# A macaron attention layer on one core: the differential softmax shared out over three engines, and the output projection as four plain products

## The chip, the core and the metric

The kernel runs on one core of one Trainium2 chip. The metric is the device time of one execution in microseconds (us), the median of a few runs. The core has TensorE (PE, matrix products; PEld is its weight load), VectorE (DVE), ScalarE (ACT), GpSimd (POOL) and SyncE (SP, which issues most DMAs). Each engine takes its instructions in the order in which the program lists them; waits between engines go through semaphores.

## The reference, cut to what matters

One layer on x of 1024 rows by 1024 columns, float32: a half-step SwiGLU block, two attentions side by side whose outputs are gated, summed and projected, and a second half-step SwiGLU block.

```python
# B: differential attention, 4 heads, two score maps per head
p = jax.nn.softmax(sc, axis=-1)
attn = p[:, :, 0] - lam * p[:, :, 1]
return jnp.einsum('bhqk,bkhe->bqhe', attn.astype(v.dtype), v)
...
g_a, g_b = jnp.split(jax.nn.sigmoid(gate_logits + b_gate[li]), 2, axis=-1)
merged = g_a * (y_a @ w_branch_a[li]) + g_b * (y_b @ w_branch_b[li])
x = x + merged @ w_o[li]
x = x + 0.5 * swiglu_ffn(rms_norm(x, ffn2_norm[li]), ffn2_w_in[li], ffn2_w_out[li])
```

Attention A has 8 heads of 64 over a band of 576 keys, attention B sees all chunks up to its own.

## The kernel before

**Products.** A float32 product is made of three reduced-precision ones: each operand is split into a high and a low part, and `mm3` (lines 129 to 133) issues hi*hi, lo*hi and hi*lo into one accumulator. The split (lines 96 to 110) is a cast on ScalarE (L100) and a difference on VectorE (L105). The large projections use the seven-product scheme of Strassen and Winograd: sums of operand blocks (A11, S1, ...; B11, T1, ...) are formed first, then seven products instead of eight.

**Order.** The framework takes the program's operations, simulates them with costs of its own, and from that sets the order on each engine and the buffer of each tile. So a change in one place can move instructions around it. The buffers that matter here are pools of fixed size: 14 `big` tiles, 10 `raw`, 10 `f`, and in PSUM 6 banks `mm` and 2 each of `tr`, `pt`, `pv`; the attention's scores take two `sc` tiles of two banks.

**Attention.** The work is cut into jobs that run as a pipeline of five (function `run`). 32 jobs of attention A (4 head pairs, 4 row blocks, 2 heads) are mixed with 16 jobs of attention B (heads 0 and 1); then come the 16 B jobs of heads 2 and 3, with steps of the branch A projection as filler. A job's first step makes scores on TensorE (L783, L784), subtracts them from the bias and takes the minimum on VectorE (L791), and takes exp and its row sum on ScalarE (L793). Two steps later the probabilities are transposed on TensorE (L799, PSUM tile `pt`), split (L100, L105), and multiplied with v (L870, L958).
- An A job has two row blocks; for each, VectorE takes the reciprocal of the row sum (L853) and GpSimd scales the probabilities (L854).
- A B job has two maps r = 0, 1 of up to 1024 keys (128, 256, ..., 1024 for its row block i = 0 to 7). VectorE takes both reciprocals (L939, L941), forms r2 = -lam * sum0 / sum1 (L942), and adds the second map to the first: pr[0] = pr[1] * r2 + pr[0] (L944). The first reciprocal is applied later, on the small result (L961, L963). GpSimd then adds the two halves (L964) and makes two small operations of the norm (L142, L970).

**Merge and output projection.** For each pair jj of 128-column blocks TensorE projects branch B (tile `pb`), VectorE gates it and adds branch A's part (L1027, L116). The result is kept in the seven operand sums that the scheme needs (A11, A12, A22 and S1 to S4): S1 and S2 are formed on VectorE, S3 and S4 on GpSimd (L1036, L1037). `out_projection` (lines 430 to 520) then does w_o in the order P1, P2, P6, P5, P3, P7, P4, four steps of 48 matmuls each, with the sums of weight blocks (T1, T2, ...) formed on VectorE between them; each product is added to the rows of x by VectorE (L510). The same function does the projections of both SwiGLU blocks, in another order.

**Behind it.** When both halves of the upper 512 rows are complete, `early` normalises them and transposes them (L208) into A11 and A12. When the lower rows are complete, `mid` and `late` do theirs: five `head`s of the next SwiGLU block, which need only A11 and A12, are issued between the normalisation of the lower rows and the sums S1, S2, S4 that the rest needs (`norm1a`).

Of the kernel before, what the change touches and what calls it, by code (L numbers as in the profile page):

```python
# [9 lines left out]
F32 = mybir.dt.float32  # L10
# [47 lines left out]
def hybrid_layer_kernel(ctx, tc, x, ffn1_norm, ffn1_w_in, ffn1_w_out, mix_norm, w_mix_in,  # L58
# [35 lines left out]
    nc.vector.memset(neg_half, -0.5)  # L94

# [257 lines left out]
    def ffn_in(w_in, u, ps, extra=None):  # L353
# [51 lines left out]
        for j, p in enumerate(pairs):  # L405
# [13 lines left out]
           "P7": ("S3", "T3", "q", 1, 1)}  # L419
    FFN_ORDER = ("P1", "P5", "P6", "P3", "P7", "P2", "P4")  # L420
    WO_ORDER = ("P1", "P2", "P6", "P5", "P3", "P7", "P4")
# [6 lines left out]
    WO_LOADS = {(0, 0): (("B11", 0, 4), ("B21", 0, 4), ("B12", 0, 4), ("B22", 0, 4))}  # L428

    def out_projection(w_out, operand, order, loads, scale, x_src, x_dst, ps,  # L430
# [5 lines left out]
        wv = w_out.rearrange("(i two p) d -> two p i d", two=2, p=P)  # L436
# [5 lines left out]
        def load_block(name, i0, i1):  # L442
            n = 2 if name == "B11" else 4
            for j0 in range(i0, i1, n):
                r = min(n, i1 - j0)
                b = raw_tile([P, 2, HALF], name) if n == 2 else big([P, 4, HALF], name, F32)
                nc.sync.dma_start(out=b[:, :r], in_=wv[int(name[1]) - 1][
                    :, j0:j0 + r, (int(name[2]) - 1) * HALF:int(name[2]) * HALF])
                for i in range(r):
                    blocks[name, j0 + i] = b[:, i, :]  # L450

        def weight(name, i):

            b11, b12, b21, b22 = (blocks.get((n, i)) for n in ("B11", "B12", "B21", "B22"))
            if order == WO_ORDER and name == "T2":
                add(b11, b12, b11, ALU.subtract)
                t2 = wtemp([P, HALF], "T2")
                add(t2, b22, b11, ALU.subtract)
                add(b21, b21, t2, ALU.subtract)
                return t2  # L460
            if order == FFN_ORDER and name in ("T1", "T2"):
# [17 lines left out]
        for m, name in enumerate(order):  # L479
# [3 lines left out]
            if first:  # L483
                banks[chain] = [ps.tile([P, HALF], F32, tag=tag, bufs=n, name="po") for tag, n in
                                (("mm", 6), ("mm", 6)) + ((("mm", 6),) * 2 if chain == "q" else (("tr", 2),) * 2)]
            if m == len(order) - 1 and last:
                early()
            for i in range(nk):
# [3 lines left out]
                if order == FFN_ORDER and bn == "B21":  # L492
# [261 lines left out]
    with tc.tile_pool(name="ps2", bufs=1, space=PSUM) as ps:  # L754
# [71 lines left out]
        def jobs_a(pr):  # L826
# [8 lines left out]
            def job(sb_, h):  # L835
# [9 lines left out]
                pms = []  # L845
                for s, i in enumerate((i0, i1)):
# [68 lines left out]
        def jobs_b(hb, filler):  # L915
# [10 lines left out]
            def job(i):  # L926
# [3 lines left out]
                pr, rs = [], []  # L930
                for r in range(2):
                    sc, n = scores(qkv, r, i, 0, w)
                    pm = raw_tile([P, WB], "pm")[:, :w]
                    s_ = small.tile([P, 1], F32, tag="rs", name="rs")
                    softmax(sc, n, nb[:, WB - w:], pm, s_)
                    pr.append(pm)
                    rs.append(s_)
# [74 lines left out]
    with tc.tile_pool(name="ps3", bufs=1, space=PSUM) as ps:  # L1012


        mo = {n: big([P, 4, HALF], f"m{n}", F32) for n in U_OPS}
        for jj in range(KT // 2):
            wr = load(w_cols(w_branch_b[0], jj * 256, 256, 0, 4), raw_tile([P, 4, 256]))
            for odd in range(2):
                j = 2 * jj + odd
                w = split_units(wr[:, :, odd * P:(odd + 1) * P], branch_unit)  # L1020
                for th in range(2):
# [6 lines left out]
                    if (odd, th) == (0, 1):  # L1028
                        a21 = ta
                    else:  # L1030
                        m = mo["A12" if odd and not th else "A22" if odd else "A11"][:, jj, :]
                    add(a21 if (odd, th) == (0, 1) else m, gl, ta)
# [69 lines left out]
```

## Time and profile before

| | us |
|---|---|
| three runs | 2160.55, 2162.82, 2162.94 (median 2162.82) |
| the profiled execution | 2162.35, of which 2160.5 are its span |
| TensorE busy | 2079.4, 96% of the span |
| VectorE, ScalarE, GpSimd busy | 1463.7, 977.7, 189.6 |

The profile is of one execution. Busy time of TensorE counts a matmul to its modelled end, so matmuls that follow each other overlap; what one costs in a row of them is the distance between two starts. A row's "idle before" names what ended the wait. Line numbers are those of the kernel before.

### The profile page before, as it was taken

How to read it: one execution, taken by the hardware profiler on the slowest of the kernel's cores; microseconds unless marked ns; L12 is line 12 of the kernel's file. 1: busy time of each engine (PE TensorE's matmuls, PEld its weight loads, DVE VectorE, ACT ScalarE, POOL GpSimd, SP SyncE). 2: the span in 40 equal slices, each digit the busy share in tenths (PEclk: the TensorE clock that was granted, in tenths of full speed). 3: DMA queues.
4: the chain of work that ended last, by engine and by line, in shares of the span. 5: the costliest groups of instructions: out<-in, count | busy, mean ns of one | idle time of the engine just before them, and what ended most of it. 6: DMA issues, size and time to landing. Idle time of an engine off the chain costs nothing.

```text
span 2160.5 us, 29119 instructions
## 1 busy us (share of the span) xinstructions
PE 2079.4 (96%) x10025; PEld 1733.3 (80%) x10025; DVE 1463.7 (68%) x2678; ACT 977.7 (45%) x1911; POOL 189.6 (9%) x290
## 2 busy tenths in 40 slices
PE   6999999999999999999988999998999999999997
PEld 5788888888888788899777787776788888888886
DVE  7666566577577756566588986777765665658566
ACT  5433333334446444444487864135433333334444
POOL 2120000000001000000065432101000000000001
PEclk9999999999999999999999999999999999999999
DMA  6653333294344645553785567614643333366334
GB/s 193 175 170 108 98 98 112 93 348 125 117 139 149 178 134 169 191 186 137 244 296 202 189 226 238 237 59 156 180 144 96 111 98 98 117 237 226 98 114 160
DMA packets 285157, 348.24 MB, mean 161 GB/s; under 512 B 16221, under 2 KB 171885, under 8 KB 284113
## 3 DMA queue, kind: packets, MB, share of 16 engines
q1 hardware_dynamic: 283680, 342.62, 48.4%
q0 software_dynamic: 1184, 3.24, 0.6%
q8 instruction: 79, 1.29, 0.3%
q14 instruction: 70, 0.57, 0.1%
q10 hardware_dynamic: 144, 0.52, 0.1%
HBM read 233.79 MB, written 112.53 MB: 160 GB/s over the span
## 4 chain that ended last, share of the span: by engine, by line
PE 81%; DVE 9%; DMA 3%; issue 3%; ACT 2%; SPq 0%; POOL 0%; ACTq 0%; DVEq 0%; POOLq 0%
PE prod L131 19%; PE prod L132 19%; PE prod L133 18%; PE po L132 6%; PE po L133 6%; PE po L131 6%; DVE wlo L105 3%; DVE pm L791 2%; PE pb L131 1%; PE pb L133 1%; PE pb L132 1%; PE tr L208 1%; DVE B L116 1%; PE pt L799 1%; ACT whi L100 1%
## 5 line engine op out<-in xcount | busy, mean ns | idle before, releaser
L132 PE MATMUL po<-wlo,whi 128*128 128x512 f32 x728 | 284.8, 391 | 5.7 <-DVE wlo L105 5.4
L133 PE MATMUL po<-whi,wlo 128*128 128x512 f32 x728 | 283.5, 389 | 0.0
L100 ACT CAST whi<-raw 128x512 fp32r<-128x512 f32 x200 | 124.4, 622 | 312.6 <-PE prod L132 245.5
L100 ACT CAST whi<-T 128x512 fp32r<-128x512 f32 x196 | 121.8, 622 | 249.8 <-PE prod L132 227.4
L100 ACT CAST whi<-B 128x512 fp32r<-128x512 f32 x178 | 110.8, 623 | 266.0 <-PE po L132 258.0
L116 DVE TENSOR_TENSOR c<-prod,c 128x512 f32<-128x512 f32 x190 | 131.1, 690 | 134.9 <-PE prod L133 122.3
L105 DVE TENSOR_TENSOR wlo<-raw,whi 128x512 fp32r<-128x512 f32 x200 | 138.6, 693 | 106.0 <-ACT whi L100 65.0
L105 DVE TENSOR_TENSOR wlo<-B,whi 128x512 fp32r<-128x512 f32 x178 | 122.4, 688 | 127.0 <-ACT whi L100 126.9
L131 PE MATMUL po<-whi 128*128 128x512 f32 x728 | 198.4, 390 | 0.5 <-DVE xc L510 0.5
L105 DVE TENSOR_TENSOR wlo<-T,whi 128x512 fp32r<-128x512 f32 x196 | 134.6, 687 | 92.5 <-ACT whi L100 91.2
L132 PEld LDWEIGHTS po<-wlo,whi 128*128 128x128 f32 x728 | 136.6, 188 | 38.1 <-DVE wlo L105 10.1
L131 PEld LDWEIGHTS po<-whi 128*128 128x128 f32 x728 | 136.2, 188 | 30.3 <-ACT whi L100 1.1
L142 POOL TENSOR_TENSOR r<-v,neg_half 128x1 f32<-128x1 f32 x64 | 45.8, 719 | 1304.2 <-DVE v L183 1226.9
L133 PEld LDWEIGHTS po<-whi,wlo 128*128 128x128 f32 x728 | 136.7, 188 | 28.0
L105 DVE TENSOR_TENSOR wlo<-N,whi 128x512 fp32r<-128x512 f32 x64 | 44.2, 690 | 114.0 <-PE prod L132 62.9
L105 DVE TENSOR_TENSOR wlo<-ha,whi 128x512 fp32r<-128x512 f32 x154 | 105.4, 684 | 9.0 <-ACT whi L100 9.0
L275 ACT COPY c<-prod 128x512 f32<-128x512 f32 x186 | 103.1, 586 | 11.4 <-DMA hA<-c 4.0
L100 ACT CAST whi<-ha 128x512 fp32r<-128x512 f32 x154 | 94.8, 615 | 16.9 <-PE prod L132 11.4
L793 ACT ACTIVATE pm<-pm,mn 128x640 f32<-128x640 f32 (+7 forms) x128 | 94.1, 737 | 13.7 <-DVE ri L941 7.3
L131 PE MATMUL prod<-A11h,whi 128*128 128x512 f32 x240 | 95.5, 398 | 2.2 <-ACT A11h L100 2.2
L131 PE MATMUL prod<-S1h,whi 128*128 128x512 f32 x240 | 94.4, 393 | 2.4 <-ACT S1h L100 1.5
L131 PE MATMUL prod<-S2h,whi 128*128 128x512 f32 x240 | 94.1, 392 | 1.3 <-ACT whi L100 1.3
(248 smaller groups left out, 5383.2 us busy)
## 6 DMA issues: line engine op xcount, KB each, us to landing
raw<-in_ffn_w_in_dram SPq DMA_DIRECT2D x98, 512.0 KB, 4.4
raw<-in_w_mix_in_dram SPq DMA_DIRECT2D x47, 512.0 KB, 4.6
ha<-hS SPq DMA_DIRECT2D x88, 256.0 KB, 2.7
hA<-c SPq DMA_DIRECT2D x66, 256.0 KB, 4.3
ha<-hA SPq DMA_DIRECT2D x66, 256.0 KB, 2.7
B<-in_ffn_w_out_dram SPq DMA_DIRECT2D x12, 1024.0 KB, 10.5
hS<-hs SPq DMA_DIRECT2D x44, 256.0 KB, 2.8
hS<-c SPq DMA_DIRECT2D x44, 256.0 KB, 4.5
```

The source lines that it names most:

```text
L100: nc.scalar.copy(out=hi, in_=src)
L105: (nc.gpsimd if on_pool else nc.vector).tensor_tensor(out=lo, in0=src, in1=h, op=ALU.subtract)
L116: nc.vector.tensor_tensor(out=out_, in0=a, in1=b, op=op)
L131: nc.tensor.matmul(ps, a[0], b[0], start=first, stop=False, skip_group_check=shared)
L132: nc.tensor.matmul(ps, a[0], b[1], start=False, stop=False, skip_group_check=shared)
L133: nc.tensor.matmul(ps, a[1], b[0], start=False, stop=last, skip_group_check=shared)
L142: nc.gpsimd.tensor_tensor(out=r, in0=v, in1=neg_half, op=ALU.pow)
L208: nc.tensor.transpose(tr[:, k, :], rows[:, k * P:(k + 1) * P], ident)
L275: nc.scalar.copy(out=self.held[name], in_=p)
L791: nc.vector.tensor_tensor_reduce(out=d3, in0=sc, in1=nb.rearrange("p (n w) -> p n w", n=n), scale=1.0, scalar=3e38, op0=ALU.add, op1=ALU.m ...
L793: nc.scalar.activation(out=dst, in_=dst, func=AF.Exp, bias=mn, scale=-1.0, accum_out=rs)
L799: nc.tensor.transpose(pt[:, b, :], p, ident)
```

## The change

In attention B the reciprocals of both sums are one GpSimd power to -1 of a 128x2 tile; ScalarE scales the second map by r2, and GpSimd adds it to the first. The three VectorE operations that did this go; the small product r2 stays on VectorE. In attention A the two reciprocals of a job become one of a 128x2 tile, after the job's second exp. The row-sum tiles have two columns, and still four buffers, so that they hold twice as much.

The output projection w_o becomes four plain sums over the eight blocks of 128, in the order W00, W01, W11, W10 (row half, column half). The merge keeps its result in four tiles, without the sums S1 to S4.

```diff
-    WO_ORDER = ("P1", "P2", "P6", "P5", "P3", "P7", "P4")
+    WO_ORDER = ("W00", "W01", "W11", "W10")
...
-    WO_LOADS = {(0, 0): (("B11", 0, 4), ("B21", 0, 4), ("B12", 0, 4), ("B22", 0, 4))}
+    WO_LOADS = {(0, 0): (("B1", 0, 8),), (0, 4): (("B2", 0, 8),)}
...
+            if plain:
+                return blocks[name, i]
             b11, b12, b21, b22 = (blocks.get((n, i)) for n in ("B11", "B12", "B21", "B22"))
-            if order == WO_ORDER and name == "T2":
-                add(b11, b12, b11, ALU.subtract)
-                t2 = wtemp([P, HALF], "T2")
-                add(t2, b22, b11, ALU.subtract)
-                add(b21, b21, t2, ALU.subtract)
-                return t2
...
-                    rs = small.tile([P, 1], F32, tag="rs", name="rs")
-                    softmax(sc, n, nb[:, h, WA - w:WA], pm, rs)
-                    ri = small.tile([P, 1], F32, tag="ri", name="ri")
-                    nc.vector.reciprocal(out=ri, in_=rs)
-                    nc.gpsimd.tensor_tensor(out=pm, in0=pm, in1=ri.to_broadcast([P, w]), op=ALU.mult)
+                    softmax(sc, n, nb[:, h, WA - w:WA], pm, rs[:, s:s + 1])
                     pms.append(pm)
+                ri = small.tile([P, 2], F32, tag="ri", name="ri")
+                nc.vector.reciprocal(out=ri, in_=rs)
+                for s, pm in enumerate(pms):
+                    nc.gpsimd.tensor_tensor(out=pm, in0=pm, in1=ri[:, s:s + 1].to_broadcast(list(pm.shape)), op=ALU.mult)
...
-                r1, r2 = (small.tile([P, 1], F32, tag="ri", name="ri") for _ in range(2))
-                nc.vector.reciprocal(out=r1, in_=rs[0])
-
-                nc.vector.reciprocal(out=r2, in_=rs[1])
-                nc.vector.scalar_tensor_tensor(out=r2, in0=r2, scalar=neg_lam, in1=rs[0],
+                ri = small.tile([P, 2], F32, tag="rj", bufs=6, name="ri")
+                nc.gpsimd.tensor_tensor(out=ri, in0=rs, in1=neg_one, op=ALU.pow)
+                r1, r2 = ri[:, 0:1], small.tile([P, 1], F32, tag="r2", name="r2")
+
+                nc.vector.scalar_tensor_tensor(out=r2, in0=ri[:, 1:2], scalar=neg_lam, in1=rs[:, 0:1],
                                                op0=ALU.mult, op1=ALU.mult)
-                nc.vector.scalar_tensor_tensor(out=pr[0], in0=pr[1], scalar=r2, in1=pr[0],
-                                               op0=ALU.mult, op1=ALU.add)
+                nc.scalar.activation(out=pr[1], in_=pr[1], func=AF.Copy, scale=r2)
+                nc.gpsimd.tensor_tensor(out=pr[0], in0=pr[0], in1=pr[1], op=ALU.add)
...
-            add(s1, a21, a22)
-            add(s2, s1, a11, ALU.subtract)
-            nc.gpsimd.tensor_tensor(out=s3, in0=a11, in1=a21, op=ALU.subtract)
-            nc.gpsimd.tensor_tensor(out=s4, in0=a12, in1=s2, op=ALU.subtract)
```

The change adds two lines near the top, so lines up to 420 of the kernel before stand two further down in the rows of the kernel after.

**GpSimd in the mixed part.** First before, around the A jobs of 384 and 512 keys (L854 scales an A job, L964, L142 and L970 belong to B jobs), then now, at the same jobs:

```order
L854 TENSOR_TENSOR pm<-pm,ri 128x384
L964 TENSOR_TENSOR o_10865<-o_10865,o_10867 128x128
L854 TENSOR_TENSOR pm<-pm,ri 128x512
L142 TENSOR_TENSOR r<-v,neg_half 128x1
L854 TENSOR_TENSOR pm<-pm,ri 128x384
L854 TENSOR_TENSOR pm<-pm,ri 128x512
```

```order
L144 TENSOR_TENSOR r<-v,neg_half 128x1
L941 TENSOR_TENSOR ri<-rs,neg_one 128x2
L972 TENSOR_TENSOR dg<-ident,r 128x128
L858 TENSOR_TENSOR pm<-pm,ri 128x384
L858 TENSOR_TENSOR pm<-pm,ri 128x512
L947 TENSOR_TENSOR pm<-pm 128x768
L858 TENSOR_TENSOR pm<-pm,ri 128x384
L858 TENSOR_TENSOR pm<-pm,ri 128x512
```

The power (L941) and the sum of 768 columns (L947) now stand among the scalings of the A jobs; the second scaling of a job follows the first at once.

**SyncE in the merge.** The loads of w_o (B) among those of the gates (gl) and of branch A's part (tA). Before, two smaller loads for the first product stand further up, and the large ones stand here, after the eighth tA:

```order
L122 DMA tA<-ta_220 128x512
L122 DMA gl<-g_213 128x512
L447 DMA B_14225<-in_w_o_dram 128x4x512
L447 DMA B_14227<-in_w_o_dram 128x4x512
L122 DMA tA<-ta_221 128x512
```

Now all four loads are large, and the first two stand after the fourteenth tA of sixteen:

```order
L124 DMA tA<-ta_225 128x512
L453 DMA B_14076<-in_w_o_dram 128x4x512
L453 DMA B_14078<-in_w_o_dram 128x4x512
L124 DMA gl<-g_218 128x512
L124 DMA tA<-ta_226 128x512
```

So the weights of the first product are asked for later than before.

**TensorE at the end of the output projection.** First before, then now (po is the projection, tr the transposes of the upper rows, prod the next block's heads):

```order
L132 MATMUL po<-wlo,whi 128x512
L133 MATMUL po<-whi,wlo 128x512
L208 MATMUL tr<-ident,xt 128x128 x16
L131 MATMUL prod<-A11h,whi 128x512
L131 MATMUL prod<-A12h,whi 128x512
```

```order
L134 MATMUL po<-wlo,whi 128x512
L135 MATMUL po<-whi,wlo 128x512
L135 MATMUL prod<-A11h,wlo 128x512
L133 MATMUL prod<-A11h,whi 128x512
L134 MATMUL prod<-A11l,whi 128x512
```

The last sixteen of the upper rows' 32 transposes stood between the projection and the heads; now all 32 stand inside the projection.

## Rows read from the trace of the kernel before

**Rows 1.** Busy time by stage: the stretch in us from the span's start and its length, then for each engine its busy us (and instructions), the clock granted to TensorE as a share of 2.4 GHz, the DMA share and GB/s. The stages are the mixed part of the attention, the rest of it with the branch projection beside it, the merge of the branches, the output projection w_o, and the 45 us behind it.

```profile
1077.00:1220.00 143.00, 127.19 (x849) 111.05 (x850) 127.42 (x413) 120.04 (x323) 87.26 (x115) 0.96 0.70 241
1220.00:1357.70 137.70, 125.49 (x750) 109.89 (x748) 105.69 (x306) 81.11 (x206) 38.37 (x73) 0.96 0.65 226
1357.70:1402.80 45.10, 41.88 (x172) 33.11 (x173) 33.50 (x49) 6.54 (x11) 8.47 (x6) 0.96 0.66 225
1402.80:1492.00 89.20, 85.05 (x374) 67.72 (x373) 70.05 (x115) 39.37 (x75) 8.03 (x6) 1.00 0.29 95
1492.00:1537.60 45.60, 37.86 (x182) 30.23 (x180) 38.75 (x67) 26.34 (x49) 3.68 (x5) 0.92 0.58 174
```

**Rows 2.** What TensorE waited for in the mixed part, 1077 to 1220 us: us in total, times, longest.

```profile
PE pt L799 <- DVE wlo L105: 4.1, 8, 1.0
PE sc L783 <- DVE mn L791: 3.6, 8, 0.9
```

**Rows 3.** The same from 1220 to 1345 us.

```profile
PE sc L783 <- DVE mn L791: 3.1, 4, 1.6
...
PE pb L131 <- ACT o L963: 2.4, 3, 1.2
...
PE pt L799 <- DVE wlo L105: 1.1, 3, 0.6
```

**Rows 4.** Groups of instructions of the whole program by line and engine: out<-in, shape, count | busy us, mean ns of one | idle time before them and what ended it.

```profile
L944 DVE SCALAR_TENSOR_TENSOR pm<-pm,ri 128x128 f32<-128x128 f32 (+7 forms) x32 | 29.6, 926 | 0.3
...
L200 ACT ACTIVATE xc<-xc,r 128x512 f32<-128x512 f32 x12 | 8.0, 712 | 0.0
...
L961 ACT ACTIVATE o<-pv,ri 128x128 f32<-128x128 f32 x32 | 11.8, 370 | 2.9 <-PE pv L959 1.9 <-POOL o L964 0.6 <-ACT whi L100 0.2
...
L142 POOL TENSOR_TENSOR r<-v,neg_half 128x1 f32<-128x1 f32 x64 | 45.8, 719 | 1304.2 <-DVE v L183 1226.9 <-DVE v L196 52.9 <-DVE v L967 18.7
...
L964 POOL TENSOR_TENSOR o<-o,o 128x128 f32<-128x128 f32 x32 | 15.8, 495 | 48.6 <-ACT o L963 48.4
...
L105 POOL TENSOR_TENSOR ya<-ysum,ya 128x256 fp32r<-128x256 f32 x16 | 11.8, 738 | 32.4 <-ACT ya L100 32.4
...
L184 DVE SCALAR_TENSOR_TENSOR xt<-xt,r,gain 128x1024 f32<-128x1024 f32 x20 | 25.6, 1279 | 1.4 <-POOL r L142 1.4
```

**Rows 5.** VectorE's groups from 1060 to 1360 us, shapes kept apart.

```profile
L791 DVE CUSTOM_DVE_ANT_0 pm<-sc,nb 128x1024 f32<-128x1024 f32 x8 | 9.7, 1215 | 0.2 <-PE pt L799 0.2
...
L944 DVE SCALAR_TENSOR_TENSOR pm<-pm,ri 128x1024 f32<-128x1024 f32 x4 | 6.1, 1517 | 0.1
...
L941 DVE RECIPROCAL ri<-rs 128x1 f32<-128x1 f32 x32 | 5.0, 156 | 0.8 <-ACT o L963 0.3 <-ACT pm L793 0.2
...
L939 DVE RECIPROCAL ri<-rs 128x1 f32<-128x1 f32 x32 | 5.0, 155 | 0.1
```

**Rows 6.** One of GpSimd's groups, shapes kept apart: the widest sum of two full tiles that it does.

```profile
L1037 POOL TENSOR_TENSOR mS<-mA,mS 128x512 f32<-128x512 f32 x4 | 5.9, 1477 | 34.3 <-DVE mS L116 34.3
```

**Rows 7.** What GpSimd waited for in the mixed part.

```profile
POOL ya L105 <- ACT ya L100: 14.9, 5, 4.6
POOL o L964 <- ACT o L963: 9.8, 3, 4.7
```

**Rows 8.** TensorE's instructions in order of time: start, duration as the profile models it, line and names.

```profile
1398.28 0.39 PE L131 MATMUL pb<-y,whi 128*128 128x512 f32 x1
1398.51 0.40 PE L132 MATMUL pb<-y,whi 128*128 128x512 f32 x1
```

**Rows 9.** SyncE's DMA issues in order of time during the merge: start, length of the issue.

```profile
1374.15 0.93 SPq L447 DMA_DIRECT2D B<-in_w_o_dram  x2
...
1388.93 0.42 SPq L122 DMA_DIRECT2D tA<-ta  x1
...
1395.88 0.32 SPq L122 DMA_DIRECT2D tA<-ta  x1
```

**Rows 10.** DMA issues from 1330 to 1500 us by kind: size of each, median us from issue to landing.

```profile
B<-in_w_o_dram SPq DMA_DIRECT2D x3, 1024.0 KB, 9.4
```

**Rows 11.** What TensorE waited for during the output projection.

```profile
PE po L132 <- DVE wlo L105: 3.3, 3, 1.5
```

**Rows 12.** TensorE at the end of the output projection, in order of time, with the idle time before an instruction and what ended it in brackets.

```profile
1491.74 0.39 PE L133 MATMUL po<-whi,wlo 128*128 128x512 f32 x1
...
1491.97 1.03 PE L208 MATMUL tr<-ident,xt 128*128 128x128 f32 x8
...
1495.73 1.57 PE L208 MATMUL tr<-ident,xt 128*128 128x128 f32 x8 [2.73 <-DVE A11l L105]
...
1498.86 0.80 PE L131 MATMUL prod<-A11h,whi 128*128 128x512 f32 x1 [1.56 <-ACT A11h L100]
```

**Rows 13.** VectorE in the same place, in order of time.

```profile
1487.73 0.68 DVE L105 TENSOR_TENSOR wlo<-mA,whi 128x512 fp32r<-128x512 f32 x1
...
1488.33 0.69 DVE L105 TENSOR_TENSOR wlo<-B,whi 128x512 fp32r<-128x512 f32 x1
...
1491.33 1.28 DVE L510 SCALAR_TENSOR_TENSOR xc<-po,xc 128x512 f32<-128x512 f32 x2
...
1505.71 0.69 DVE L105 TENSOR_TENSOR wlo<-raw,whi 128x512 fp32r<-128x512 f32 x1 [3.65 <-ACT whi L100]
...
1539.58 0.69 DVE L105 TENSOR_TENSOR S4l<-tr,S4h 128x512 fp32r<-128x512 f32 x1 [0.63 <-ACT S4h L100]
```

More of the change, by code (lines that the diff above doesn't have):

```diff
@@ L94, in hybrid_layer_kernel @@
     nc.vector.memset(neg_half, -0.5)
+    neg_one = const.tile([P, 2], F32, name="neg_one")
+    nc.vector.memset(neg_one, -1.0)
     def split(src, hi, lo, scale=None, on_pool=False):
@@ L446, in load_block @@
                 b = raw_tile([P, 2, HALF], name) if n == 2 else big([P, 4, HALF], name, F32)
-                nc.sync.dma_start(out=b[:, :r], in_=wv[int(name[1]) - 1][
-                    :, j0:j0 + r, (int(name[2]) - 1) * HALF:int(name[2]) * HALF])
+                dh = int(name[-1]) - 1
+                nc.sync.dma_start(out=b[:, :r], in_=wv[0 if plain else int(name[1]) - 1][
+                    :, j0:j0 + r, dh * HALF:(dh + 1) * HALF])
                 for i in range(r):
@@ L452, in weight @@
         def weight(name, i):
+            if plain:
+                return blocks[name, i]
             b11, b12, b21, b22 = (blocks.get((n, i)) for n in ("B11", "B12", "B21", "B22"))
-            if order == WO_ORDER and name == "T2":
-                add(b11, b12, b11, ALU.subtract)
-                t2 = wtemp([P, HALF], "T2")
-                add(t2, b22, b11, ALU.subtract)
-                add(b21, b21, t2, ALU.subtract)
-                return t2
-            if order == FFN_ORDER and name in ("T1", "T2"):
+            if name in ("T1", "T2"):
                 add(b11, b12 if name == "T1" else b22, b11, ALU.subtract)
@@ L491, in out_projection @@
                 steps.append((split_units(operand(an, i)), split_units(weight(bn, i))))
-                if order == FFN_ORDER and bn == "B21":
+                if bn == "B21":
                     add(blocks[bn, i], blocks[bn, i], blocks["B11", i], ALU.subtract)
@@ L845, in job @@
                 pms = []
+                rs = small.tile([P, 2], F32, tag="rs", bufs=4, name="rs")
                 for s, i in enumerate((i0, i1)):
@@ L929, in job @@
                 w = (i + 1) * P
-                pr, rs = [], []
+                pr = []
+                rs = small.tile([P, 2], F32, tag="rs", name="rs")
                 for r in range(2):
@@ L1012, in hybrid_layer_kernel @@
     with tc.tile_pool(name="ps3", bufs=1, space=PSUM) as ps:
-        mo = {n: big([P, 4, HALF], f"m{n}", F32) for n in U_OPS}
+        mo = {(th, g): big([P, 4, HALF], f"m{th}{g}", F32) for g in range(2) for th in range(2)}
         for jj in range(KT // 2):
@@ L1027, in hybrid_layer_kernel @@
                     nc.vector.tensor_tensor(out=gl, in0=pb, in1=gl, op=ALU.mult)
[L1028 to L1032, printed above, removed]
-            a11, a12, a22, s1, s2, s3, s4 = (mo[n][:, jj, :] for n in ("A11", "A12", "A22", "S1", "S2", "S3", "S4"))
-            add(s1, a21, a22)
-            add(s2, s1, a11, ALU.subtract)
-            nc.gpsimd.tensor_tensor(out=s3, in0=a11, in1=a21, op=ALU.subtract)
-            nc.gpsimd.tensor_tensor(out=s4, in0=a12, in1=s2, op=ALU.subtract)
+                    add(mo[th, j // 4][:, j % 4, :], gl, ta)
         gain = load_gain(ffn2_norm[0])
@@ L1040, in hybrid_layer_kernel @@
         ffn2 = ffn_in(ffn2_w_in[0], u3, ps)
[L1041 removed]
+        out_projection(w_o[0], lambda n, i: mo[int(n[1]), i // 4][:, i % 4, :], WO_ORDER, WO_LOADS, 1.0, x_mid, x_mix, ps,
                        *renorm(x_mix, gain, u3, ps, ffn2))
```

14 lines of the change are left out of this document (7 added, 7 removed).

## The prediction

> **What bounds the kernel now.** I read the busy times by stage first, then what TensorE waits for in each stage the change touches, then the order on each engine. Busy times by stage show TensorE near its limit everywhere, 85 of 89 us in the output projection, and the attention as the one place where four engines are loaded at once: in the mixed part's 143 us VectorE is busy 127.4, TensorE 127.2, ScalarE 120.0, GpSimd 87.3 [rows 1]. TensorE's waits there name VectorE twice at the top, for splits of transposed probabilities and for the minimum that frees a score tile: 4.1 and 3.6 us [rows 2]. So VectorE ends most waits there, with ScalarE 7 us behind it. In the second stretch TensorE is busy 125.5 of 137.7 and ScalarE only 81.1 [rows 1], and waits on the same two VectorE groups make 4.2 us [rows 3]. The granted clock of 0.96 in both [rows 1] says that some of these pauses are followed by time at the 1.2 GHz level. Everything before 1077 us keeps its order on TensorE, and so does everything from some 30 us behind the output projection's tail; I count nothing there.
>
> **The softmax: what leaves and what arrives.** In attention B VectorE loses 32 sums of two maps, mean 0.926 us [rows 4], and 64 reciprocals of 0.155 [rows 5]; in A 32 of 64 reciprocals of the same size. Half of the B jobs lie in each stretch, all A jobs in the first. First stretch: 16 x 0.926 + 32 x 0.155 + 32 x 0.155 = 24.7 us less, so 102.7. Second: 14.8 + 5.0 = 19.8 less, so 85.9.
>
> ScalarE gains 32 scalings of mean width 576 (128 to 1024 in eight steps). Its scaled copies cost 0.712 us at 512 columns and 0.370 at 128 [rows 4], so 0.89 ns a column and 0.77 us at 576: 12.3 us more in each stretch. First stretch 132.3 us, second 93.4.
>
> GpSimd gains 32 sums and 32 powers. Its sums of two full tiles take 0.495 us at 128 columns and 0.738 at 256 [rows 4], 1.9 ns a column, so 1.35 us at 576; the 512-column row of 1.477 [rows 6], taken beside busy VectorE work, would make it 1.6. A power of two columns stands in no row. One column takes 0.719 us [rows 4]; two take at least about that and at most twice, 1.44. I take 0.72, the nearest row, and keep 1.44. First stretch: 16 x (1.35 + 0.72) = 33.1 us more, so 120.4, or 131.9 at the upper price. Second: 71.5 of 137.7, no limit.
>
> A VectorE sum whose inputs both lie in SBUF runs longer beside GpSimd: 1.517 us at 1024 columns in the attention [rows 5] against 1.279 elsewhere [rows 4]. The bias step, which reads PSUM and SBUF, stays at 1.215 there [rows 5]. If every remaining VectorE instruction were stretched like that sum, by 19%, the first stretch's 102.7 would become 122, still under ScalarE's 132; with none stretched it stays 102.7. The term is the same, so I add nothing for it. The Trainium skill, page "SBUF — State Buffer", section "Who interferes with whom", says that a VectorE instruction with two SBUF inputs and a GpSimd instruction that reads SBUF exclude each other for a whole instruction, while one SBUF input does not contend. That speaks against putting more sums on GpSimd; by it VectorE stays at 102.7 plus what its few two-input splits and squares lose. These rows agree.
>
> **First stretch: what is late next.** The busiest engine goes from VectorE's 127.4 to ScalarE's 132.3. The stretch was 15.6 us longer than its busiest engine; kept, that makes 147.9, 4.9 us more. Against it: TensorE's 7.7 us of waits on VectorE go at least half, about 4. The scalings wait for a chain that now crosses four engines (exp, power, r2, scaling, sum). In the new order such a scaling stands several instructions behind its exp, and behind it wait the casts of the next transposes, but the transposes themselves come two job steps later, so I cost the longer chain at nothing while GpSimd has slack. I take +1; ends -6 (waits on VectorE nearly all go) and +13 (rival 2).
>
> **Second stretch.** TensorE is the limit and loses VectorE waits of 4.2 us plus their slow-clock tail. GpSimd and ScalarE have room. I take -3; ends -8 and +2, the latter if the last jobs' longer chains show.
>
> **The output projection.** It goes from 7 x 4 to 4 x 8 steps of 12 matmuls: 48 more (four row blocks, three each). Starts are 0.23 us apart [rows 8], about 10.9 us in a row. Nothing hides it, since TensorE is busy 85.05 of 89.2 us [rows 1]. VectorE loses 16 weight sums, 8 operand sums and 12 additions to rows and gains 8 splits: 28 fewer at 0.60 us between starts [rows 13], 17 us over merge and projection. Its part in TensorE's waits here is 3.3 us [rows 11], which I let go as 3. Sixteen transposes move in, 8 in 1.03 us [rows 12]: 2.1. The projection grows by 10.9 + 2.1 - 3 = 10; ends +7 and +13.
>
> *Its start.* Before, the first product's weights were loaded ahead of the merge. Now the first two loads stand behind the fourteenth tA load. At the pace of before that is issued at 1388.93 [rows 9], and a load takes 9.4 us to land [rows 10]: 1398.3, and 1399.6 with a cast and a difference. TensorE has 172 projection matmuls ahead of it from 1357.7, 39 us, to 1396.8. The start was 1402.8, so -3; I take -2. If the loads slip to the fifteenth, 1395.88 [rows 9], the start is 1406.6, +4; the other end is -4.
>
> *Its tail.* Before, the upper rows were complete after five of seven products, 22 us before the end, and their normalisation ran into the end of w_o: the last sixteen transposes waited 2.73 us for a split and the first head 1.56 for a cast [rows 12], and the clock of the 45 us behind is 0.92 [rows 1]. Now those rows are complete after two of four products, over 43 us ahead, and all 32 transposes lie inside. What is left behind the end is VectorE's chain for the lower rows. From the first addition at 1491.33 to the last split of S4, 1539.58 + 0.69, it took 48.9 us [rows 13]. The order lists 65 wide instructions in it, 39 us at 0.60; the rest is waits, the largest 3.65 us for a cast that stood behind slow TensorE [rows 13]. Now it lists 60, 36 us. With 4 us of waits that is 40, so I take -8; ends -11 (no wait left) and -3 (only the five instructions go).
>
> Merge, projection and tail: -2 + 10 - 8 = 0. The products added cost what the earlier normalisation gives back.
>
> **Sum.** +1 - 3 + 0 = -2 us. The profiled execution took 2162.35 us, 1.85 more than its span and 0.5 under the median of the three, 2162.82. Forecast: 2160.3 us.
>
> **Rivals.**
> 1. *VectorE's relief comes through whole.* For it: it is named first in both stretches, and the row-sum tiles, now twice as deep, no longer hold back an exp. All of 7.7 + 4.2 us goes, w_o still even: 2162.35 - 11.9 = 2150.5. Against it: ScalarE at 132 of 143.
> 2. *GpSimd becomes the limit of the mixed part.* The power costs 1.44, so GpSimd is busy 131.9; its waits for ScalarE in its own order, 14.9 + 9.8 us [rows 7], do not shrink, since the sums wait there too. Together 156.6 against 143: +13.6. With -3 behind it, 2173. It decides once busy time and those waits pass 143 plus the 4 us that VectorE gives back. Against it: at 0.72 the same sum is 145, and it had long idle stretches.
> 3. *The tail is not paid back.* The lower rows' chain alone sets the restart, heads or not: tail -3, projection +13, start +2, so +12, with the softmax's -2: 2172. For it: VectorE was 85% busy behind the projection [rows 1]. Against it: the 3.65 us hole, which had TensorE's slow restart ahead of it.
>
> **How the numbers follow.** Chances: forecast 0.45, spread 2156 to 2165; rival 1 0.28; rival 2 0.16; rival 3 0.11. A measurement of this kernel tells 0.2%, 4.3 us, from no change: faster is below 2158.5, slower above 2167.1. Of the forecast's 0.45 I count 0.14 faster, 0.28 same, 0.03 slower. So faster 0.42, same 0.28, slower 0.30. The range 2150 to 2173 reaches to all three rivals and leaves their outer halves out.
>
> **What would show it.** Right: in the mixed part VectorE near 103 us, ScalarE near 132, GpSimd near 120, and TensorE's waits on VectorE halved; the projection's first to last matmul 10 us longer, no wait before the first head, S4's last split about 40 us behind the projection. Wrong: a GpSimd sum at the head of TensorE's waits, a power of 1.4 us, ScalarE waiting for r2, or TensorE waiting for the first weights of w_o.

## The result, and the profile after

| | median us | runs |
|---|---|---|
| before, on the same occasions | 2159.69 | 13 |
| changed | 2167.33 | 13 |

The ratio is 1.0044, 95% interval 1.003 to 1.0057: the changed kernel is 9.5 us slower (below, every difference is the ratio less one, times 2159.5 us). The forecast was 2160.3, a shade faster; 2167.33 lies inside the range given, 2150 to 2173, but on the other side of no change. The profiled execution took 2168.69 us, span 2166.5, 6.0 more than before.

Busy time by stage after the change, with the bounds and columns of [rows 1]:

```profile
1077.00:1220.00 143.00, 123.93 (x818) 107.45 (x819) 115.81 (x337) 121.72 (x319) 98.48 (x131) 0.96 0.67 230
1220.00:1357.70 137.70, 122.71 (x744) 106.33 (x744) 87.90 (x243) 95.79 (x232) 84.76 (x113) 0.98 0.56 191
1357.70:1402.80 45.10, 42.55 (x192) 34.34 (x191) 25.81 (x45) 7.96 (x18) 3.42 (x7) 1.00 0.74 244
1402.80:1492.00 89.20, 88.18 (x403) 72.36 (x402) 61.59 (x99) 43.60 (x82) 2.85 (x4) 1.00 0.45 157
1492.00:1537.60 45.60, 44.07 (x208) 35.91 (x207) 36.44 (x63) 26.41 (x50) 4.97 (x5) 1.00 0.48 148
```

In the mixed part TensorE did less than before (123.93 us against 127.19) although VectorE has 11.6 us less to do. No engine is full over the stretch (ScalarE is busy 85% of it, GpSimd 69%): the loss is one of waiting. TensorE's waits there, in the columns of [rows 2]:

```profile
PE sc L785 <- DVE mn L793: 5.5, 11, 1.6
PE pv L873 <- ACT whi L102: 2.1, 3, 1.0
PE pt L801 <- DVE yb L109: 2.0, 3, 1.3
PE pt L801 <- DVE wlo L107: 1.9, 3, 1.3
```

The splits of transposed probabilities fell from 4.1 to 1.9 us. The minimum that frees a score tile rose from 3.6 to 5.5, and two others rose beside it whose work begins on ScalarE: the cast `whi`, from 0.6 to 2.1, and `yb`, a difference that follows an instruction of ScalarE's, from 0.7 to 2.0. The new instructions themselves, by shape, cost what was worked out from [rows 4, 6], GpSimd's sums a little more; first GpSimd's, then ScalarE's:

```profile
L941 POOL TENSOR_TENSOR ri<-rs,neg_one 128x2 f32<-128x2 f32 x32 | 22.5, 704 | 7.9 <-ACT pm L795 7.5 <-DMA nb<-diag_a 0.4
...
L947 POOL TENSOR_TENSOR pm<-pm 128x1024 f32<-128x1024 f32 x4 | 9.5, 2381 | 4.8 <-ACT pm L946 4.8
```

```profile
L946 ACT ACTIVATE pm<-pm,r 128x1024 f32<-128x1024 f32 x4 | 4.6, 1140 | 0.0
```

The power of two columns takes 0.704 us, no more than one column. The eight shapes of the sum have a mean of 1.44 us, those of the scaling 0.77.

How such a pause arises can be read in one place, 1168 to 1190 us. The engines in order of time, ScalarE first, then VectorE, GpSimd and TensorE; columns as in [rows 12]:

```profile
1168.62 1.04 ACT L946 ACTIVATE pm<-pm,r 128x896 f32<-128x896 f32 x1
1169.56 0.35 ACT L104 ACTIVATE yb<-try,gsub 128x128 fp32r<-128x128 f32 x1
...
1181.88 1.15 ACT L946 ACTIVATE pm<-pm,r 128x1024 f32<-128x1024 f32 x1
1182.94 0.35 ACT L102 CAST whi<-pt 128x256 fp32r<-128x256 f32 x1
```

```profile
1169.94 0.35 DVE L109 SCALAR_TENSOR_TENSOR yb<-try,gsub,yb 128x128 fp32r<-128x128 f32 x1 [1.33 <-ACT yb L104]
...
1174.03 1.23 DVE L793 CUSTOM_DVE_ANT_0 pm<-sc,nb 128x1024 f32<-128x1024 f32 x1 [0.51 <-POOL pm L947]
...
1175.18 1.35 DVE L969 CUSTOM_DVE_ANT_0 sq<-o 128x128 f32<-128x128 f32 x1
```

```profile
1175.12 2.51 POOL L858 TENSOR_TENSOR pm<-pm,ri 128x640 f32<-128x640 f32 x2
...
1183.11 2.36 POOL L947 TENSOR_TENSOR pm<-pm 128x1024 f32<-128x1024 f32 x1 [3.21 <-ACT pm L946]
```

```profile
1170.35 0.55 PE L801 MATMUL pt<-ident,pm 128*128 128x128 f32 x3 [1.32 <-DVE yb L109]
...
1177.73 0.41 PE L785 MATMUL sc<-ks,qs 128*128 128x320 f32 x1 [1.57 <-DVE mn L793]
...
1183.34 0.33 PE L873 MATMUL pv<-whi,vt 128*128 128x128 f32 x1 [1.00 <-ACT whi L102]
```

Twice a scaling of over 1 us, whose result TensorE does not need yet, stands on ScalarE ahead of a short instruction (`yb`, then the cast `whi`) whose result it needs next; the pauses are 1.32 and 1.00 us. For the second scaling GpSimd has waited 3.21 us, with two scalings of branch A behind that sum in its queue. Between the two pauses VectorE waits 0.51 us for a buffer that GpSimd's sum still uses, and then its square of 128 columns takes 1.35 us beside GpSimd's scalings, so that the next minimum comes late: 1.57 us. Behind these three pauses the clock falls to the 1.2 GHz level; the columns are those of [rows 1]:

```profile
1180.00:1185.00 5.00, 3.50 (x23) 2.59 (x22) 3.29 (x9) 4.88 (x11) 1.89 (x1) 0.95 0.94 366
1185.00:1190.00 5.00, 4.83 (x21) 4.56 (x22) 2.32 (x5) 1.58 (x4) 3.58 (x4) 0.50 1.04 392
```

The output projection's ends, on TensorE, and S4's last split on VectorE, for [rows 12, 13]:

```profile
1407.53 0.62 PE L133 MATMUL po<-whi 128*128 128x512 f32 x2
...
1502.70 0.39 PE L133 MATMUL prod<-A11h,whi 128*128 128x512 f32 x1
...
1504.74 0.39 PE L135 MATMUL po<-whi,wlo 128*128 128x512 f32 x1
```

```profile
1545.76 0.69 DVE L107 TENSOR_TENSOR S4l<-tr,S4h 128x512 fp32r<-128x512 f32 x1 [0.63 <-ACT S4h L102]
```

The first product starts 4.7 us later than before (1402.83), the projection takes 97.6 us to the end of its last matmul instead of 89.3, the tail to the end of S4's last split 41.3 instead of 48.1: +4.7 + 8.3 - 6.8 = +6.2, the span's 6.0. The first head lies inside the projection, without a wait.

Those 4.7 us are what is left of a larger delay. TensorE's last transposes of branch B's output (`try`), and its first product of w_o, both before; then the transposes now:

```profile
1353.18 0.61 PE L974 MATMUL try<-dg,o 128*128 128x128 f32 x4
...
1402.83 0.39 PE L131 MATMUL po<-whi 128*128 128x512 f32 x1
```

```profile
1365.34 0.60 PE L976 MATMUL try<-dg,o 128*128 128x128 f32 x4
```

They start 12.2 us later, with 172 matmuls of the branch projections left behind them in the trace where 185 were left before, some 3 us of work at 0.23 us each. So by this estimate the attention is 9 us late, and the merge gives back 4 to 5 of them.

### The profile page after: what moved, and what is told of

It reads as the page before. It is cut to its first block, busy times and chain, and to the rows that moved or that the text cites. A ratio compares the mean times of both kernels' runs of the same rounds, so it can differ in the third digit from the quotient of the medians.

```text
span 2166.5 us, 29144 instructions
## 1 busy us (share of the span) xinstructions
PE 2086.5 (96%) x10073; PEld 1740.2 (80%) x10073; DVE 1421.3 (66%) x2523; ACT 1000.7 (46%) x1951; POOL 239.2 (11%) x346
## 5 line engine op out<-in xcount | busy, mean ns | idle before, releaser
L134 PE MATMUL po<-wlo,whi 128*128 128x512 f32 x744 | 290.9, 391 | 2.9 <-DVE wlo L107 2.9
L135 PE MATMUL po<-whi,wlo 128*128 128x512 f32 x744 | 289.5, 389 | 0.0
L102 ACT CAST whi<-B 128x512 fp32r<-128x512 f32 x186 | 115.8, 623 | 272.3 <-PE po L134 263.5
L107 DVE TENSOR_TENSOR wlo<-B,whi 128x512 fp32r<-128x512 f32 x186 | 128.2, 689 | 140.0 <-ACT whi L102 140.0
L793 DVE CUSTOM_DVE_ANT_0 pm<-sc,nb 128x640 f32<-128x640 f32 (+7 forms) x128 | 87.8, 703 | 22.5 <-PE pt L801 11.5
```

The lines of the kernel that those rows point to most:

```text
L102: nc.scalar.copy(out=hi, in_=src)
L107: (nc.gpsimd if on_pool else nc.vector).tensor_tensor(out=lo, in0=src, in1=h, op=ALU.subtract)
L134: nc.tensor.matmul(ps, a[0], b[1], start=False, stop=False, skip_group_check=shared)
L135: nc.tensor.matmul(ps, a[1], b[0], start=False, stop=last, skip_group_check=shared)
L793: nc.vector.tensor_tensor_reduce(out=d3, in0=sc, in1=nb.rearrange("p (n w) -> p n w", n=n), scale=1.0, scalar=3e38, op0=ALU.add, op1=ALU.m ...
```

## Experiments

**The two halves.** The first run has the softmaxes of the changed kernel and the old w_o, the second the reverse.

```diff
 first, against the changed kernel:
-    WO_ORDER = ("W00", "W01", "W11", "W10")
+    WO_ORDER = ("P1", "P2", "P6", "P5", "P3", "P7", "P4")
...
 second, against the changed kernel:
-                nc.scalar.activation(out=pr[1], in_=pr[1], func=AF.Copy, scale=r2)
-                nc.gpsimd.tensor_tensor(out=pr[0], in0=pr[0], in1=pr[1], op=ALU.add)
+                nc.vector.scalar_tensor_tensor(out=pr[0], in0=pr[1], scalar=r2, in1=pr[0],
+                                               op0=ALU.mult, op1=ALU.add)
...
```

> The kernel before with the whole change of the softmaxes (branch A's one reciprocal a job, branch B's power, scaling and sum), and w_o in its seven products as before. Theory S (the loss is in the attention: a longer chain over four engines and a GpSimd that is full in the mixed part): 4 to 8 us above the kernel before, nearly the whole loss of the changed kernel. Rival W (the loss comes in with w_o, by its later loads at the merge or by its 48 more matmul steps): -4 to +1 us. Rival I (the two only cost together, since the merge's fillers run out): 0 to +3 us.

> The kernel before with w_o as four plain products and the softmaxes as before. By the changed kernel's trace the projection grows by 8.1 us and its tail shrinks by 6.6. Theory S: -2 to +3 us against the kernel before. Rival W: 5 to 9 us above it. Rival I: 0 to +3 us.

Measured: the softmaxes alone 1.0061 (1.0046 to 1.0076), +13.2 us; w_o alone 0.9968 (0.9956 to 0.998), -6.9 us. Theory S's sign holds, but both numbers lie outside what was written: the changed kernel is a loss of 13 to 16 us of which a gain of 7 hides a part.

**Link by link.** Three runs take the changed kernel's B softmax back in parts.

```diff
 first:
-                nc.gpsimd.tensor_tensor(out=ri, in0=rs, in1=neg_one, op=ALU.pow)
+                nc.vector.reciprocal(out=ri, in_=rs)
 second:
-                nc.scalar.activation(out=pr[1], in_=pr[1], func=AF.Copy, scale=r2)
-                nc.gpsimd.tensor_tensor(out=pr[0], in0=pr[0], in1=pr[1], op=ALU.add)
+                nc.vector.scalar_tensor_tensor(out=pr[0], in0=pr[1], scalar=r2, in1=pr[0], ...
 third:
-                nc.gpsimd.tensor_tensor(out=pr[0], in0=pr[0], in1=pr[1], op=ALU.add)
+                nc.vector.tensor_tensor(out=pr[0], in0=pr[0], in1=pr[1], op=ALU.add)
```

> The changed kernel with one instruction of branch B's softmax moved back: the reciprocals of both row sums are one VectorE reciprocal of 128x2 (0.16 us) in place of GpSimd's power (0.70 us, and a hop between engines). ScalarE still scales, GpSimd still adds. If the loss is GpSimd's load and the hop: 2 to 5 us below the changed kernel. If the loss is elsewhere (w_o, or the later place of the sum): within 1.5 us of it.

> The changed kernel with the power kept on GpSimd, but the second map scaled and added by one VectorE instruction again, as before: ScalarE loses some 25 us, GpSimd some 46 us, VectorE gains some 30. If the later sum (ScalarE, then GpSimd at 2.3 ns a column) costs the attention its time: 4 to 8 us below the changed kernel. If the power and its hop cost it: within 2 us of the changed kernel. If VectorE was the limit: 2 to 6 us above it.

> The changed kernel with only the engine of the sum of the two maps changed: ScalarE still scales the second map, VectorE adds (two inputs in SBUF), the power stays on GpSimd. Theory G (GpSimd's sum is the dear part: 1.44 us a job in the mean, 46 us in all, on an engine that has other links of the chain to do): 7 to 12 us below the changed kernel, near the kernel with the whole sum on VectorE, which is 15 us below it. Rival A (ScalarE's scaling is the dear part: 25 us more on an engine that was 120 of 143 us busy, and one hop more): 0 to 4 us below the changed kernel.

Measured against before: without the power 1.0026 (1.0012 to 1.0039), +5.6 us; with the sum on VectorE 0.9974 (0.9961 to 0.9988), -5.6; scaled by ScalarE and added by VectorE 1.002 (1.001 to 1.003), +4.3. So the power costs 4 us of the 9.5 (uncertain by as much); scaling and sum together cost 15, about twice what was written; and with the scaling left on ScalarE, only 5 of these come back (uncertain by 3.6), between the bands of theory G and rival A. That last run has VectorE add behind ScalarE, with 7.1 us of waits for it:

```profile
DVE pm L947 <- ACT pm L946: 7.1, 10, 1.2
```

**Where.** The new B softmax in heads 0 and 1 only (mixed part), or in heads 2 and 3 only; the other heads have two VectorE reciprocals and the VectorE sum.

```diff
+                if hb < 2:        # second run: hb >= 2
...
+                else:
+                    nc.vector.reciprocal(out=r1, in_=rs[:, 0:1])
+                    nc.vector.reciprocal(out=ri[:, 1:2], in_=rs[:, 1:2])
...
```

> The changed kernel with the new softmax of branch B (power, ScalarE, GpSimd) only in heads 0 and 1, which lie in the mixed part; heads 2 and 3 have the two VectorE reciprocals and the VectorE sum as before. Against the kernel before the changed kernel is 9.5 us slower, and w_o alone is 6.9 us faster, so the new softmaxes cost some 16 us beside the new w_o. If they cost it in the mixed part, where GpSimd is busy 98 of 143 us: this kernel is 5 to 9 us above the kernel before. If in the second stretch, where the last jobs' chain is in the open: -7 to -2 us below it. If in both alike: -1 to +3 us.

> The other half: the new softmax of branch B only in heads 2 and 3, heads 0 and 1 as before. If the mixed part bears the cost: 7 to 2 us below the kernel before. If the second stretch bears it: 5 to 9 us above. If both alike: -1 to +3 us. If the two halves add up, this run and the one with heads 0 and 1 together stand some 3 us above twice the kernel before.

Measured: 1.0009 (0.9996 to 1.0021), +1.9 us, and 0.9979 (0.9969 to 0.9989), -4.5 us. Set against w_o alone, the mixed part costs 8.8 us and the second stretch 2.4; both together, in the changed kernel, 16.4. The mixed part bears most of it, but neither number fell in the band written for it. The 2.4 is uncertain by 3.4, and the 5 us that appear only with both by as much as their size.

**One reciprocal for two maps, the rest on VectorE.** This keeps A's one reciprocal a job and w_o in plain products.

```diff
-                nc.gpsimd.tensor_tensor(out=ri, in0=rs, in1=neg_one, op=ALU.pow)
+                nc.vector.reciprocal(out=ri, in_=rs)
-                nc.scalar.activation(out=pr[1], in_=pr[1], func=AF.Copy, scale=r2)
-                nc.gpsimd.tensor_tensor(out=pr[0], in0=pr[0], in1=pr[1], op=ALU.add)
+                nc.vector.scalar_tensor_tensor(out=pr[0], in0=pr[1], scalar=r2, in1=pr[0], ...
```

> The changed kernel without its moves to other engines: branch B's sum is VectorE's again, and one VectorE reciprocal of 128x2 does for both maps; branch A's one reciprocal a job and w_o in four plain products stay. Against w_o alone (6.9 us below the kernel before) VectorE loses 64 small instructions, some 10 us. If VectorE's load ends TensorE's waits in the attention: 9 to 13 us below the kernel before. If the load of VectorE was covered: 5 to 9 us below. If A's single reciprocal costs time, since the first map's scaling now waits for the second map's exp: 2 to 6 us below.

Measured: 0.9969 (0.9959 to 0.9979), -6.7 us, within 3.4 us the same as w_o alone. 64 reciprocals fewer on VectorE, and one reciprocal a job in branch A, gave and cost nothing that can be seen: this much of VectorE's load was covered. This kernel, as w_o alone, beats both.

**Load without the chain.** From here the base is that last kernel, B8 (-6.7). ScalarE's scalings, or GpSimd's sums, come back as work into a scrap tile whose contents nobody waits for; two controls have the same instructions with one column each. The outputs don't depend on them.

```diff
+                nc.scalar.activation(out=junk[:, :w], in_=pr[1], func=AF.Copy, scale=r2)
                 nc.vector.scalar_tensor_tensor(out=pr[0], in0=pr[1], scalar=r2, in1=pr[0], ...
 or, behind it:
+                nc.gpsimd.tensor_tensor(out=junk[:, :w], in0=pr[0], in1=pr[1], op=ALU.add)
 controls: [:, :1] for all operands
```

> The kernel with one reciprocal and the whole sum on VectorE (6.7 us below the kernel before) with ScalarE's 32 scalings of the second map put back as work that nobody waits for: each writes a scrap tile, and VectorE forms the sum as in that kernel. ScalarE gets the 25 us, no link of the chain moves. Theory L (ScalarE's load: its scalings stand in its queue ahead of the casts that free transposed tiles): most of the 10 us that the scaling cost on its own, so 0 to +4 us against the kernel before. Rival C (the chain: the sum comes later since it waits for another engine): within 2.5 us of the kernel that it is made from, -9 to -4.5 us.

> The control for the run with ScalarE's load alone: the same 32 scalings into the scrap tile at the same place in the program, with the same waits, but of one column each (about 0.2 us in place of 0.4 to 1.15). That run stood 9 us above the kernel that it is made from, and the framework also gave it another order on every engine. If the load on ScalarE is what costs: -7 to -3 us against the kernel before, 5 to 9 below the run with full columns. If the mere presence of the instruction (its wait for r2, the other order) costs: 0 to +4 us.

> The same kernel with GpSimd's 32 sums put back as work that nobody waits for: VectorE forms the sum, then GpSimd adds the two maps once more into a scrap tile (about 46 us of work, which keeps both maps' buffers that much longer). If GpSimd's load costs (its scalings for branch A and its diagonals stand behind the sums, and VectorE's instructions with two operands in SBUF run longer beside it): +3 to +7 us above the kernel that it is made from, -4 to 0 us against the kernel before. If only the chain through GpSimd cost: within 2 us of the kernel that it is made from, -9 to -5 us.

> The control for the run with GpSimd's load alone: the same 32 sums into the scrap tile, at the same place and with the same waits, of one column each (some 0.5 us in place of 0.46 to 2.38). If the load on GpSimd is what costs: -7 to -3 us against the kernel before, 5 to 9 below the run with full columns. If the presence of the instruction, its hold on the buffers or the other order costs: 0 to +4 us.

| B8 and | ratio to before (95%) | us against before | against B8 |
|---|---|---|---|
| ScalarE's scalings, full | 1.0012 (0.9998 to 1.0025) | +2.6 | +9.3 |
| the same, one column | 0.9989 (0.9979 to 1.0) | -2.4 | +4.3 |
| GpSimd's sums, full | 1.001 (0.9999 to 1.0022) | +2.2 | +8.9 |
| the same, one column | 0.9971 (0.9959 to 0.9982) | -6.3 | +0.4 |

GpSimd's sums cost 9 us by their load alone, more than the 3 to 7 written: nobody waits for their result, and with one column (0.20 us each) they cost nothing, though the framework gave that control, too, another order than B8's. How the load reaches TensorE is not taken apart. Instructions behind the sums come later: TensorE waits 1.5 us for a diagonal of GpSimd's (`dg`) in the full run's trace. VectorE waits 1.9 us for buffers that the sums hold (0.6 in the control's trace). And VectorE's small product r2, all of whose inputs lie in SBUF, runs longer, in the full run and then in the control:

```profile
L944 DVE SCALAR_TENSOR_TENSOR r<-ri,neg_lam,rs 128x1 f32<-128x1 f32 x32 | 12.7, 398 | 0.1
```

```profile
L944 DVE SCALAR_TENSOR_TENSOR r<-ri,neg_lam,rs 128x1 f32<-128x1 f32 x32 | 8.7, 271 | 0.1
```

ScalarE's cost 9 us too, but some half stays with one column, between the two bands written for that control (each of these two halves is uncertain by over 3 us). The control's instruction still takes 0.29 us, 9.4 in all, and ScalarE stands in its queue until r2 comes. In the control, in the run with full columns and in the changed kernel (three traces, 1077 to 1360 us) that wait is:

```profile
ACT junk L946 <- DVE r L944: 7.0, 4, 3.6
```

```profile
ACT junk L946 <- DVE r L944: 6.4, 7, 2.3
```

```profile
ACT pm L946 <- DVE r L944: 8.0, 5, 4.9
```

Whether the control's 4 us are this wait, the 0.29 us or the order is open. The profiled execution of the full run was its fastest of twelve, 2156.32 us, no slower than B8's, 2156.83; so its trace does not show where its time goes.

**VectorE scales, GpSimd adds**, on B8:

```diff
-                nc.vector.scalar_tensor_tensor(out=pr[0], in0=pr[1], scalar=r2, in1=pr[0], ...
+                nc.vector.tensor_scalar(out=pr[1], in0=pr[1], scalar1=r2, scalar2=None, op0=ALU.mult)
+                nc.gpsimd.tensor_tensor(out=pr[0], in0=pr[0], in1=pr[1], op=ALU.add)
```

> The same kernel with the second map scaled by VectorE (one input in SBUF, in place) and added by GpSimd: the chain's last link on GpSimd, but no ScalarE in it, and the reciprocal on VectorE. If the costs add up (the scaling on ScalarE 10 us, the sum on GpSimd 5, the power 1 to 4): -4 to 0 us against the kernel before. If GpSimd's sum is dear only behind ScalarE's scaling: -9 to -5 us. If VectorE's load decides: it gives up some 10 us of work against the kernel that it is made from, and should be faster than -7 us.

Measured: 1.0008 (0.9998 to 1.0018), +1.7 us, 8.4 above B8 and 0.5 below the run with GpSimd's load alone, both uncertain by over 3 us. So as a link of the chain the sum costs no more than as mere load, as far as can be seen: VectorE has some 10 us less to do here, and what that is worth beside a loaded GpSimd was not measured by itself. The sum was dearer than the 5 us written for it. The parts do not add up: the sum's 9, the scaling's 9 and the power's 4 are more than the 16 that the new softmaxes cost beside the new w_o.

**Why w_o alone gains 7 us.** In its trace the first product starts 10.0 us earlier than before, at 1392.82. SyncE's issues of the kernel before, and then of w_o alone, columns as in [rows 9]:

```profile
1329.96 0.39 SPq L447 DMA_DIRECT2D B<-in_w_o_dram  x1
...
1333.27 0.38 SPq L447 DMA_DIRECT2D B<-in_w_o_dram  x1
...
1336.73 2.00 SPq L122 DMA_DIRECT2D xc<-xm  x3
...
1339.25 2.70 SPq L122 DMA_DIRECT2D xc<-xm  x4
```

```profile
1381.16 0.99 SPq L451 DMA_DIRECT2D B<-in_w_o_dram  x2
...
1384.25 2.17 SPq L122 DMA_DIRECT2D x<-xm  x4
```

Before, 3 MB of weights and rows went out from 1330 to 1342 us, among the gate tiles (`gl`) of the last branch projections; now they follow some 50 us later. Three stretches of the kernel before, and the same of w_o alone, columns as in [rows 1]:

```profile
1330.00:1340.00 10.00, 8.60 (x37) 6.93 (x38) 5.56 (x20) 3.29 (x10) 2.70 (x6) 0.83 1.01 350
1340.00:1350.00 10.00, 8.04 (x42) 6.55 (x41) 4.00 (x13) 3.51 (x11) 4.15 (x10) 0.99 0.99 350
1350.00:1360.00 10.00, 8.79 (x34) 6.86 (x34) 3.22 (x6) 1.24 (x3) 0.95 (x2) 0.84 0.92 343
```

```profile
1330.00:1340.00 10.00, 8.78 (x50) 7.38 (x49) 6.72 (x21) 3.28 (x10) 3.03 (x6) 1.00 0.74 264
1340.00:1350.00 10.00, 9.38 (x47) 7.80 (x46) 3.36 (x12) 2.91 (x9) 4.77 (x10) 1.00 0.65 198
1350.00:1360.00 10.00, 8.39 (x39) 6.67 (x39) 6.11 (x11) 2.39 (x5) 0.00 (x0) 1.00 0.92 318
```

TensorE gets through 136 matmuls there (not all of one size) instead of 113: the DMA engines are less full, and the clock stays at 2.4 GHz. That VectorE waited less for the gate tiles the traces do not show: from 1320 to 1365 us it waited 3.5 us for them before and 6.4 in w_o alone. The test puts two of the weight loads back ahead of the merge, 2 MB, in w_o alone:

```diff
+        for j0 in (0, 4):
+            b = big([P, 4, HALF], "B1", F32)
+            nc.sync.dma_start(out=b, in_=w_o[0].rearrange("(i p) d -> p i d", p=P)[:, j0:j0 + 4, 0:HALF])
+            for i in range(4):
+                early_b1["B1", j0 + i] = b[:, i, :]
         for jj in range(KT // 2):
```

> The kernel with the old softmaxes and w_o as four plain products (6.9 us below the kernel before), with the first two loads of w_o's weights (2 x 1 MB) issued before the merge's first tile of branch A, some 45 us earlier, where the kernel before issued two loads of 0.5 MB and eight of 0.25 MB of rows. If w_o alone gained its time there (in its trace the first product starts 10 us earlier, the DMA engines are 0.65 to 0.94 busy from 1320 to 1350 where they were 0.97 to 1.01, and the clock is 1.00 where it was 0.83 to 0.99): 3 to 7 us of the gain are lost, -4 to 0 us against the kernel before. If the gain comes from VectorE's and GpSimd's missing operand sums in the merge: -8 to -5 us.

Measured: 0.9986 (0.9973 to 1.0), -3.0 us: 3.9 of the 6.9 are lost again, uncertain by as much, and one stretch is back at the clock of before:

```profile
1330.00:1340.00 10.00, 9.12 (x41) 7.23 (x39) 4.28 (x17) 2.77 (x8) 2.58 (x5) 0.83 0.98 371
```

That clock alone proves little: B8's trace, with late loads, has 0.83 from 1320 to 1330 us and from 1340 to 1350. So that the early loads cost time is likely, and the way by which they do is open.

The other 3 us were not taken apart by a run, but the trace before shows a place in the merge. VectorE, then TensorE:

```profile
1384.11 1.29 DVE L116 TENSOR_TENSOR B<-B,B 128x512 f32<-128x512 f32 x2 [2.14 <-DMA B<-in_w_o_dram]
...
1388.45 1.75 DVE L105 TENSOR_TENSOR wlo<-raw,whi 128x512 fp32r<-128x512 f32 x1
```

```profile
1390.25 0.49 PE L133 MATMUL pb<-y,wlo 128*128 128x512 f32 x1 [1.99 <-DVE wlo L105]
```

A sum of weight blocks, which only the seven products need, waits 2.14 us for its load at the head of VectorE's queue; behind it stand the operand sums and a split, for which TensorE then waits 1.99 us, and the clock of 1390 to 1400 us is 0.83. In w_o alone these sums do not exist, TensorE's waits for such splits from 1320 to 1405 us are 0.6 us instead of 3.2, and the run with the early loads keeps that.

## Why the prediction was wrong

**First stretch, +1: failed, and with it the sign.** The step "I cost the longer chain at nothing while GpSimd has slack" compared sums of busy time: ScalarE 132 of 143, GpSimd 120. In its place the runs show a cost of the new softmaxes of 16 us beside the new w_o (13 beside the old), most of it in this stretch. The unit costs were right (power 0.70 for 0.72, scaling 0.77 for 0.77, sum 1.44 for 1.35), and no engine became full. What it left out is the place in the queue: on ScalarE, 85% busy, a 1 us instruction that is not urgent stands ahead of short ones that TensorE waits for, as the two pauses above show. The prediction had seen casts behind a scaling, but took them for those of transposes two job steps away; in the trace above what stands behind it is work that TensorE uses within half a microsecond of its end. As load alone GpSimd's instructions, up to 2.4 us long on an engine 69% busy, cost 9 us; ScalarE's cost 9, of which some half is theirs by length.

The expected busy times did not appear in the window (ScalarE 121.7, GpSimd 98.5, VectorE 115.8). "Half of the B jobs lie in each stretch" was a wrong reading: up to 1220 us the trace before has 11 of the 32 sums, not 16, and the trace now 10; before, in the columns of [rows 4]:

```profile
L944 DVE SCALAR_TENSOR_TENSOR pm<-pm,ri 128x128 f32<-128x128 f32 (+7 forms) x11 | 11.3, 1024 | 0.0
```

And whole durations were taken off a busy time in which neighbours overlap: the rows of VectorE's groups there add up to 153 us before, with 127.4 busy, and to 132 now, so that 21 us of rows were 11.6 of busy time.

**VectorE's relief: worth nothing.** I let 4 us of TensorE's waits on VectorE go in the first stretch and 3 in the second. The two groups that made 7.7 us in the first still make 7.4. Taking 64 reciprocals from VectorE changed nothing that can be seen (0.2 us, uncertain by 3.4). VectorE ended most waits, but what made it late was often ScalarE's cast before it, and with the change it still is; VectorE's waits from 1077 to 1220 us, before and now:

```profile
DVE wlo L105 <- ACT whi L100: 9.0, 12, 1.9
```

```profile
DVE wlo L107 <- ACT whi L102: 10.1, 13, 1.9
```

The second stretch lost 2.4 us (uncertain by 3.4) instead of gaining 3, about the upper end, +2, given there.

**Rival 2** had the right engine and the right part of the program for about half of the loss, but its condition, a power of 1.44 us, did not hold; GpSimd cost its 9 us without being the limit. Rival 1 is refuted. A GpSimd sum at the head of TensorE's waits, named as the sign of failure, is not there; ScalarE waiting for r2, the other sign, is: 8.0 us.

**The start of w_o, -2: wrong in the changed kernel, 4.7 us later, beyond the upper end, +4.** The late attention brings it there. By itself the new w_o has the sign forecast, and a larger size: in w_o alone the start came 10.0 us earlier. The term was sized by when the new loads land, [rows 9, 10]; what the old loads and the operand and weight sums cost where they were stands in no term.

**The projection, +10, and the tail, -8: right.** Measured +8.3 and -6.8 in the changed kernel; with w_o alone 96.0 us, +6.7, and 40.7, -7.4. With w_o alone the projection lies just below the lower end given, +7; which of its terms was too large was not taken apart. Rival 3 is refuted.

The Trainium skill, page "SBUF — State Buffer", section "Who interferes with whom", was cited for two-input VectorE instructions and GpSimd excluding each other; the trace agrees in single places: the square `sq` of 128 columns took 0.27 to 0.29 us in most of its 32 cases, and 1.35 beside the GpSimd scalings above. So "I add nothing for it" left out a term, a small one: 32 squares cost 12.8 us instead of 10.3, and 32 small products r2 11.0 instead of 7.2; and one such square made a minimum 1.1 us late.

## What to carry to other kernels

Before moving work to a less busy engine, look at what is queued behind it there: a long instruction that is not urgent can cost time if short instructions on the path of the bounding engine stand behind it, before the engine is full. Measure the load by itself, as work into a scrap tile, beside a control of one column. And when loads move, ask first what they held up where they were.

## What was not expected of the hardware

Between some kernels the mean clock granted over the span goes with the loss. It was 0.9922 in the mean of 23 runs of the kernel before, 0.9948 with w_o alone (5 runs), 0.9945 in B8 (11), 0.9916 in the changed kernel (13). If TensorE has work all through, 1 - 0.9922 of 2160 us is 16.8 us lost at the lower level; by the same estimate 11.2 with w_o alone, 11.8 in B8, 18.2 in the changed kernel. By this estimate some 6 us of the 16 between the changed kernel and B8, and most of w_o's gain, go with the clock: a pause can be paid for a second time behind it, as the 5 us at 0.50 above. But it is no rule between kernels: without the power the mean clock is 0.9942 (12 runs), above the kernel before's, and that kernel is 5.6 us slower. Within one kernel the two go together: the run with ScalarE's full scalings took 2156.32 us at 0.995 and 2167.74 at 0.989.
